# Input projection by block products: the forget gate's place among the token sums, a later split of a11 − a21, and the pace of the attention steps

## The chip, the cores and the metric

The kernel runs on one core of a Trainium2 chip. The metric is the device time of one execution in microseconds (us), less is better; a kernel's time is the median over several runs. The engines are PE (TensorE, matrix products), DVE (VectorE), ACT (ScalarE), POOL (GpSimd) and SP (SyncE, which issues most transfers).

## What is computed

One decoder block over 512 tokens of width 2048, in float32. A gated linear attention (four heads) and a differential softmax attention (four heads) share one input projection; their concatenated results go through one output projection, and a gated MLP with a short convolution follows.

```python
proj = h @ w_in                                  # 512 x 2048 by 2048 x 6160
gq, gk, gv, gg, ga, dq, dk, dv = ...             # columns of proj
log_a = jax.nn.log_sigmoid(ga @ w_alpha_up + b_alpha) / GLA_TAU
o_a = gla_chunked(gq, gk, gv, log_a)             # 4 heads, chunks of 64 tokens
o_a = rmsnorm(o_a, gla_norm) * silu(gg)
o_b = diff_attention(dq, dk, dv, lam)            # 4 heads, query blocks of 128, causal
o_b = rmsnorm(o_b, diff_norm) * (1.0 - lambda_init)
m = concatenate([o_a, o_b]) @ w_o
x = x + rmsnorm(m, attn_post_norm)
x = x + rmsnorm(conv_ffn(rmsnorm(x, ffn_pre_norm)), ffn_post_norm)
```

## The kernel before

**Products.** Every float32 operand is held as two parts, a rounded high part and the rest. ACT copies to the high part and DVE subtracts to get the low part; a product is three matmuls (high by high, low by high, high by low). The normed tokens lie as `ah` and `al` for the whole phase. Weights come as granules of 128 x 1024 numbers (`raw`, 512 KB): `granule` copies one on ACT (L137) and subtracts it on DVE (L138) into one of the slots of `ring`, and PE then runs the granule's matmuls. `split` (L150 on ACT, L151 on DVE) does the same for tokens.

**Block products.** The first columns of the input projection (gv's first half, gq's and gk's first halves) are plain products (L173 to L175 for the last of them). The other columns go through ten units of 512 columns (`InUnit`). A unit views tokens and weights as 2 x 2 blocks and takes seven block products, in the order x0, z0, y0, z1, x1, y1, y2 (y2 after the next unit's x0), where four products use sums of token blocks and sums of weight blocks. A segment has two granules of 24 matmuls each of 256 columns (L695 to L697 or L699 to L701). The weight blocks `b22` of y0 and z1 are fetched into "rm" buffers by SP (L48), and L720 adds them on DVE to the blocks that z0 used.

**Token sums.** `in_sums` makes, for each of two halves of the tokens' blocks, q = s5 (used in z0), then s2 (y0) and s3 (z1) from it in place, and r = a11 − a21 (L416 to L418). These run on 128 x 1024 tiles on DVE. r's split (to `sums["s7"]`, for y1) overwrites the rows of `ah` and `al` that hold a21, so it must come behind all uses of a21. q, r, and `b22` are all "rm" tiles, of which there are two.

**Forget gate.** `forget_gate` loads 16 columns of weights (`gar`), splits them into `gas`, multiplies (L439, L440: 32 matmuls), copies to `gaT`, multiplies by the second weight (L448), and computes the log of the sigmoid for four heads: Abs (L452), Exp (L457) and Ln (L459) on ACT, minimum (L453) and subtraction (L462) and a running sum (L463, a scan) on DVE; the sums go to DRAM (`bcd`). Its four `za` tiles are 128 x 512, in the "qk" pool with four buffers.

**Fillers.** The attention work is written as generators in the list `fill`: `in_sums`, `forget_gate`, then `gla_head` (14 steps each) and `diff_head` (8 steps each: a load, then a pipeline of `probs`, `turn`, `values` and `store` over four query blocks). `step()` is called after each granule; it adds `pace[0]` to a counter and runs one step of the first generator for every whole number. `drain()` runs all that is left. In `gla_head` the matmuls L510 and L502 are the scores (L502 is called the level products below) and DVE's L489 to L495 make their operands. In `diff_head` L589 makes scores on PE, L605 ends the softmax on DVE, L612 transposes it, L614 copies it on ACT, L620 multiplies by the values, L623 and L626 norm the result, L632 transposes it and L634 copies it (`dst`).

**What sets the order.** Each engine runs its instructions in a fixed order. In this phase a scheduler sets it when the kernel is built: it takes the instructions in the order written, with a simulated time line, and may move an instruction ahead of one that waits. PE's queue is in order, so an attention product whose operand is late stops the granules behind it. Behind the last unit the output projection follows (L191 to L193), which begins with the slots of the differential heads (`place_diff`, split by L150 and L151) and takes the gate's slots (`turn_gate`, transposes L781) last.

Of the kernel before, what the change touches and what calls it, by code (L numbers as in the profile page):

```python
# [9 lines left out]
F32 = mybir.dt.float32  # L10
F32R = mybir.dt.float32r
U8 = mybir.dt.uint8
AF = mybir.ActivationFunctionType
# [4 lines left out]
P = 128  # L18
D = 2048
S = 512  # L20
# [15 lines left out]
def hybrid_layer(ctx: ExitStack, tc: tile.TileContext, x, attn_pre_norm, w_in, w_alpha_up, b_alpha,  # L36
# [10 lines left out]
    def dma(o, i):  # L47
        return nc.sync.dma_start(out=o, in_=i)  # L48
# [3 lines left out]
    act = nc.scalar.activation  # L52
# [20 lines left out]
    ah = const.tile([P, NT, KT, P], F32R, name="ah")  # L73
    al = const.tile([P, NT, KT, P], F32R, name="al")
    wpool = ctx.enter_context(tc.tile_pool(name="w", bufs=3))

    def bank(pool=None):
        return (pool or psa).tile([P, 512], F32, name="bank", tag="bank")

    fill = []  # L80
    pace = [0.0, 0.0]
# [67 lines left out]
    def split(hi, lo, src):  # L149
        act(hi, src, AF.Copy)  # L150
        tt(lo, src, hi.bitcast(F32), ALU.subtract)  # L151
# [44 lines left out]
    def proj_n(w3, col, emit, order=tuple(range(KT)), first=0, banks=None):  # L196
        if banks is None:
            banks = [bank(psm) for _ in range(NT)]
        for g in range(first, KT // 2):
            w = granule(w3[:, order[2 * g]:order[2 * g] + 2, col:col + 512], 2)  # L200
            for t in range(NT):
                mm_n(banks, t, g, w)
                if g == KT // 2 - 1:
                    emit(t, banks[t])
            step()
# [99 lines left out]
    HK = KT // 2  # L305
# [21 lines left out]
    def wide(name):  # L327
        return mx.tile([P, GR], F32, name=name, tag="rm", bufs=2)

    def block_tile(name):  # L330
        return mx.tile([P, 512], F32, name=name, tag="ub", bufs=5)

    def qk_tile(name):
        return mx.tile([P, S], F32, name=name, tag="qk", bufs=4)

    def tmp(name):
        return mx.tile([P, S], F32, name=name, tag="tmp", bufs=4)

    def quarter(name):
        return mx.tile([P, 256], F32, name=name, tag="w1", bufs=3)  # L340
# [6 lines left out]
    for li, hs in enumerate(LEVELS):  # L347
        nb = 64 // hs
        m = quarter("m")[:, :64]
# [38 lines left out]

    s7raw = []

    def in_sums():
        for i in range(2):
            def blk(r, c):
                return [v[:, 2 * r + i, HK * c:HK * (c + 1), :].bitcast(F32) for v in (ah, al)]

            a11, a12, a21, a22 = blk(0, 0), blk(0, 1), blk(1, 0), blk(1, 1)

            def flat(name):
                return wide(name).rearrange("p (k c) -> p k c", c=P)

            q = flat("q")
            tt(q, a21[0], a22[0], ALU.subtract)
            tt(q, q, a21[1], ALU.add)
            tt(q, q, a22[1], ALU.subtract)
            split(sums["s5"][0][:, i], sums["s5"][1][:, i], q)
            yield
            tt(q, q, a11[0], ALU.subtract)
            tt(q, q, a11[1], ALU.subtract)
            split(sums["s2"][0][:, i], sums["s2"][1][:, i], q)
            yield  # L410
            tt(q, q, a12[0], ALU.add)
            tt(q, q, a12[1], ALU.add)
            split(sums["s3"][0][:, i], sums["s3"][1][:, i], q)
            yield
            r = flat("r")
            tt(r, a11[0], a21[0], ALU.subtract)  # L416
            tt(r, r, a11[1], ALU.add)
            tt(r, r, a21[1], ALU.subtract)  # L418
            s7raw.append(r)
            yield  # L420

    def forget_gate():
        gar = quarter("gar").rearrange("p (k r) -> p k r", r=RANK)
        dma(gar, w_in3[:, :, C_GA:C_GA + RANK])
        gas = mx.tile([P, KT, 80], F32R, name="gas", tag="v", bufs=1)
        nc.gpsimd.memset(gas.bitcast(F32), 0.0)
        split(gas[:, :, 0:RANK], gas[:, :, 64:64 + RANK], gar)
        wup = block_tile("wup")[:80, :]
        nc.gpsimd.memset(wup, 0.0)
        dma(wup[0:RANK, :], w_alpha_up[0])  # L430
        dma(wup[64:64 + RANK, :], w_alpha_up[0])
        keep = block_tile("keep")
        nc.gpsimd.memset(keep, 1.0)
        nc.gpsimd.memset(keep.rearrange("p (c x) -> p c x", c=4)[:, :, 0:1], 0.0)
        yield
        gab = bank()
        gav = gab[:80, :].rearrange("p (t c) -> p t c", c=P)
        for k in range(KT):
            mm(gav, gas[:, k, :], ah[:, :, k, :], start=k == 0, stop=False)  # L439
            mm(gav, gas[:, k, :], al[:, :, k, :], start=False, stop=k == KT - 1)  # L440
        gaT = block_tile("gaT")[:80, :]
        nc.vector.tensor_copy(gaT, gab[:80, :])
        yield

        za, bt = [], []
        for h in range(GH):
            zb = bank()
            mm(zb, wup[:, h * P:(h + 1) * P], gaT, start=True, stop=True)  # L448
            bcol = cols[:, h:h + 1]
            za.append(qk_tile("za"))  # L450
            bt.append(tmp("bt"))
            act(za[h], zb, AF.Abs, bias=bcol)  # L452
            ts(bt[h], zb, bcol, 0.0, ALU.add, ALU.min)  # L453
            if h % 2:
                yield
        for m in za:
            act(m, m, AF.Exp, scale=-1.0)  # L457
        for m in za:
            act(m, m, AF.Ln, bias=1.0)  # L459
        yield  # L460
        for h, m in enumerate(za):
            tt(m, bt[h], m, ALU.subtract)  # L462
            nc.vector.tensor_tensor_scan(bt[h], keep, m, 0.0, ALU.mult, ALU.add)  # L463
            dma(bcd[h], bt[h])
            if h % 2:
                yield
# [282 lines left out]
    def rows_unit(col, dst):  # L749
        def done(j, i, u):  # L750
            dma(dst[:, 2 * i:2 * i + 2, 256 * j:256 * (j + 1)], two(u))

        return InUnit(False, (col, col + 256), done)

    def pair_unit(c0, c1, d0, d1):
        def done(j, i, u):
            dma((d0, d1)[j][:, :, 256 * i:256 * (i + 1)], two(u))

        return InUnit(True, (c0, c1), done)
# [46 lines left out]
    def plain_out(d):  # L806
        def emit(n, b):
            u = block_tile("qk0")
            act(u, b, AF.Copy)
            dma(d[0][:, n, :], u)  # L810
        return emit

    units = [rows_unit(C_GV + 512, gvd[1]), pair_unit(C_GQ + 256, C_GK + 256, gqd[1], gkd[1])]
# [5 lines left out]
            units.append(pair_unit(C_DQ + 256 * h, C_DK + 256 * h, dqd[h], dkd[h]))  # L819
    units += [gate_unit(0), gate_unit(1)]  # L820

    fill.extend((in_sums(), forget_gate()))
    pace[0] = 1.35
    proj_n(w_in3, C_GV, gv_out, first=4, banks=banks)
    proj_t(w_in3, C_GQ, plain_out(gqd))
    banks = [bank(psm) for _ in range(2)]
# [6 lines left out]
        step()  # L833
    for n in range(2):
        plain_out(gkd)(n, banks[n])
    for i, r in enumerate(s7raw):
        split(sums["s7"][0][:, i], sums["s7"][1][:, i], r)
    fill.extend((gla_head(0), gla_head(1)))
    pace[:] = 0.62, 0.0
    units[0].z0()  # L840
    for i, u in enumerate(units):
        u.y0()
        u.z1()
# [23 lines left out]
    m = [wp.tile([P, D], F32, name=f"m{t}") for t in range(NT)]  # L867
# [722 lines left out]
```

## Time and profile before

| | us |
|---|---|
| runs | 2126.39, 2127.74, 2123.69 (median 2126.39) |
| profiled execution, its own time | 2123.57 |
| its span | 2121.9 |
| PE busy in the span | 2071.5 |
| DVE busy | 1539.2 |
| ACT busy | 988.8 |
| POOL busy | 287.8 |

The mean granted PE clock of the profiled execution is 0.994. Rows of a timeline give start, duration, engine, line, operation and tiles; a bracket at the end tells how long the engine was idle before the row and who ended that wait. Rows of the windows view give a stretch, its length, the busy time (and count) of PE, PE's weight loads, DVE, ACT and POOL, then PE's granted clock, the share of the DMA engines and GB/s. PE's matmuls overlap in the pipeline, so durations are longer than the distance between starts, which is what PE takes for one.

### The profile page before, as it was taken

How to read it: one execution, taken by the hardware profiler on the slowest of the kernel's cores; microseconds unless marked ns; L12 is line 12 of the kernel's file. 1: busy time of each engine (PE TensorE's matmuls, PEld its weight loads, DVE VectorE, ACT ScalarE, POOL GpSimd, SP SyncE). 2: the span in 40 equal slices, each digit the busy share in tenths (PEclk: the TensorE clock that was granted, in tenths of full speed). 3: DMA queues.
4: the chain of work that ended last, by engine and by line, in shares of the span. 5: the costliest groups of instructions: out<-in, count | busy, mean ns of one | idle time of the engine just before them, and what ended most of it. 6: DMA issues, size and time to landing. Idle time of an engine off the chain costs nothing.

```text
span 2121.9 us, 35562 instructions
## 1 busy us (share of the span) xinstructions
PE 2071.5 (98%) x14449; PEld 1907.2 (90%) x14449; DVE 1539.2 (73%) x1844; ACT 988.8 (47%) x1274; POOL 287.8 (14%) x306
## 2 busy tenths in 40 slices
PE   7999999999989999999999999999999999999998
PEld 6789999999967889899999999999999878787886
DVE  5867676666754246787786787878777778888887
ACT  4364444455653234344554544454444554444433
POOL 0212122222200000011111111111110110110100
PEclk9999999999999999999999999999999999999999
DMA  5567877898755345356757667577676876676653
GB/s 208 132 166 180 191 180 181 178 197 198 177 161 185 102 145 171 122 126 158 176 135 191 152 152 189 137 169 179 145 168 176 222 223 175 182 188 165 171 164 142
DMA packets 280697, 358.61 MB, mean 169 GB/s; under 512 B 14592, under 2 KB 221876, under 8 KB 278612
## 3 DMA queue, kind: packets, MB, share of 16 engines
q1 hardware_dynamic: 195732, 261.95, 36.6%
q0 software_dynamic: 84800, 94.38, 29.4%
q8 instruction: 113, 1.85, 0.4%
q14 instruction: 52, 0.43, 0.1%
HBM read 311.72 MB, written 44.56 MB: 168 GB/s over the span
## 4 chain that ended last, share of the span: by engine, by line
issue 54%; PE 34%; POOL 4%; DVE 3%; ACT 2%; DMA 2%; POOLq 0%; SPq 0%; DVEq 0%; ACTq 0%
PE bank L695 3%; PE bank L697 3%; PE bank L696 3%; PE bank L192 3%; PE bank L191 3%; PE bank L193 3%; PE bank L699 3%; PE bank L701 3%; PE bank L700 3%; POOL rt L1118 2%; POOL raw L1118 2%; PE bank L502 1%; DVE ring L138 1%; PE bank L589 1%; PE bank L175 1%
## 5 line engine op out<-in xcount | busy, mean ns | idle before, releaser
L137 ACT ACTIVATE ring<-raw 128x1024 fp32r<-128x1024 f32 x325 | 343.7, 1060 | 538.8 <-PE bank L1171 116.1
L138 DVE TENSOR_TENSOR ring<-raw,ring 128x1024 fp32r<-128x1024 f32 x325 | 395.6, 1221 | 230.9 <-ACT ring L137 230.7
L1172 PE MATMUL bank<-ah,ring 128*128 128x256 f32 x1280 | 353.5, 276 | 0.7 <-DVE ring L138 0.7
L1170 PE MATMUL bank<-ah,ring 128*128 128x256 f32 x1280 | 353.3, 276 | 0.0
L1171 PE MATMUL bank<-al,ring 128*128 128x256 f32 x1280 | 353.3, 276 | 0.0
L137 ACT ACTIVATE ring<-rt 128x1024 fp32r<-128x1024 f32 x221 | 233.0, 1059 | 226.8 <-PE bank L1171 143.8
L138 DVE TENSOR_TENSOR ring<-rt,ring 128x1024 fp32r<-128x1024 f32 x221 | 268.8, 1220 | 90.2 <-ACT ring L137 90.0
L1172 PEld LDWEIGHTS bank<-ah,ring 128*128 128x128 f32 x1280 | 240.2, 188 | 0.9 <-DVE ring L138 0.9
L1170 PEld LDWEIGHTS bank<-ah,ring 128*128 128x128 f32 x1280 | 240.2, 188 | 0.1
L1171 PEld LDWEIGHTS bank<-al,ring 128*128 128x128 f32 x1280 | 240.2, 188 | 0.1
L1273 PE MATMUL bank<-ring,ah 128*128 128x512 f32 x424 | 166.6, 393 | 4.3 <-DVE ring L138 4.2
L1274 PE MATMUL bank<-ring,al 128*128 128x512 f32 x424 | 165.2, 390 | 0.0
L1272 PE MATMUL bank<-ring,ah 128*128 128x512 f32 x424 | 159.0, 392 | 2.0 <-ACT ring L137 1.2
L191 PE MATMUL bank<-ring,ah 128*128 128x512 f32 x280 | 110.1, 399 | 4.0 <-ACT ah L150 3.9
L192 PE MATMUL bank<-ring,ah 128*128 128x512 f32 x280 | 110.5, 396 | 0.4 <-DVE ring L138 0.4
L193 PE MATMUL bank<-ring,al 128*128 128x512 f32 x280 | 108.1, 394 | 0.0
L1118 POOL DMA_DIRECT2D raw<-in_w_ffn_in_dram x40 | 51.0, 1278 | 405.4 <-DVE ring L138 402.5
L1273 PEld LDWEIGHTS bank<-ring,ah 128*128 128x128 f32 x424 | 79.6, 188 | 25.5 <-DVE ring L138 9.4
L1272 PEld LDWEIGHTS bank<-ring,ah 128*128 128x128 f32 x424 | 79.3, 188 | 21.6 <-ACT ring L137 4.9
L1118 POOL DMA_DIRECT2D rt<-in_w_ffn_in_dram x40 | 50.9, 1274 | 320.1 <-DVE ring L138 258.4
L1274 PEld LDWEIGHTS bank<-ring,al 128*128 128x128 f32 x424 | 79.6, 188 | 16.3
L695 PE MATMUL bank<-ah,ring 128*128 128x256 f32 x320 | 91.4, 285 | 0.0
(348 smaller groups left out, 5680.7 us busy)
## 6 DMA issues: line engine op xcount, KB each, us to landing
raw<-in_w_ffn_in_dram SPq DMA_DIRECT2D x96, 512.0 KB, 5.4
raw<-in_w_in_dram SPq DMA_DIRECT2D x56, 512.0 KB, 5.8
raw<-in_w_ffn_out_dram SPq DMA_DIRECT2D x48, 512.0 KB, 5.9
raw<-in_w_in_dram POOLq DMA_DIRECT2D x40, 512.0 KB, 6.7
rt<-in_w_ffn_in_dram SPq DMA_DIRECT2D x40, 512.0 KB, 6.1
rt<-in_w_ffn_in_dram POOLq DMA_DIRECT2D x40, 512.0 KB, 6.1
raw<-in_w_ffn_in_dram POOLq DMA_DIRECT2D x40, 512.0 KB, 7.7
raw<-in_w_o_dram SPq DMA_DIRECT2D x32, 512.0 KB, 4.0
```

The source lines that it names most:

```text
L137: act(hi, raw, AF.Copy)
L138: tt(lo, raw, hi.bitcast(F32), ALU.subtract)
L191: mm(banks[t], ah[:, t, s, :], w[0][:, k, :], start=st, stop=False)
L192: mm(banks[t], ah[:, t, s, :], w[1][:, k, :], start=False, stop=False)
L193: mm(banks[t], al[:, t, s, :], w[0][:, k, :], start=False, stop=sp)
L1118: nc.gpsimd.dma_start(out=raws[g].rearrange("p (a b) -> p a b", a=self.a), in_=self.block(0, j, g), accum_op=ALU.add)
L1170: mm(o, wh, sh[:, :, kk, :], start=start and kk == 0 and n == 0, stop=False, **NOW)
L1171: mm(o, wh, sl[:, :, kk, :], start=False, stop=False, **NOW)
L1172: mm(o, wl, sh[:, :, kk, :], start=False, stop=kk == HK - 1, **NOW)
L1272: mm(b[j], sh[:, o:o + P], w[0][:, q, :], start=start and st == 0, stop=False, **NOW)
L1273: mm(b[j], sh[:, o:o + P], w[1][:, q, :], start=False, stop=False, **NOW)
L1274: mm(b[j], sl[:, o:o + P], w[0][:, q, :], start=False, stop=st == 3, **NOW)
```

## The change

`in_sums` is cut in two: `first_sums` makes s5 and s2, `last_sums` makes s3 and r. `forget_gate` stands first in `fill`, ahead of both. Its four `za` tiles become halves of two 128 x 1024 tiles from the "rm" pool, so that Exp and Ln run as two instructions each. The pace of the first phase goes from 1.35 to 1.6, that of the attention steps from 0.62 to 0.75. The split of r moves from ahead of the first unit's z0 to behind it. Lines from `forget_gate`'s logs on stand 7 further down in the changed kernel (L720 becomes L727, L589 becomes L596, and so on).

```diff
--- before.py
+++ after.py
@@ -388,16 +388,18 @@
 
     s7raw = []
 
-    def in_sums():
+    def flat(name):
+        return wide(name).rearrange("p (k c) -> p k c", c=P)
+
+    def in_blocks(i):
+        return [[v[:, 2 * r + i, HK * c:HK * (c + 1), :].bitcast(F32) for v in (ah, al)]
+                for r in range(2) for c in range(2)]
+
+    s3raw = []
+
+    def first_sums():
         for i in range(2):
-            def blk(r, c):
-                return [v[:, 2 * r + i, HK * c:HK * (c + 1), :].bitcast(F32) for v in (ah, al)]
-
-            a11, a12, a21, a22 = blk(0, 0), blk(0, 1), blk(1, 0), blk(1, 1)
-
-            def flat(name):
-                return wide(name).rearrange("p (k c) -> p k c", c=P)
-
+            a11, a12, a21, a22 = in_blocks(i)
             q = flat("q")
             tt(q, a21[0], a22[0], ALU.subtract)
             tt(q, q, a21[1], ALU.add)
@@ -407,7 +409,12 @@
             tt(q, q, a11[0], ALU.subtract)
             tt(q, q, a11[1], ALU.subtract)
             split(sums["s2"][0][:, i], sums["s2"][1][:, i], q)
+            s3raw.append(q)
             yield
+
+    def last_sums():
+        for i, q in enumerate(s3raw):
+            a11, a12, a21, a22 = in_blocks(i)
             tt(q, q, a12[0], ALU.add)
             tt(q, q, a12[1], ALU.add)
             split(sums["s3"][0][:, i], sums["s3"][1][:, i], q)
@@ -442,21 +449,21 @@
         nc.vector.tensor_copy(gaT, gab[:80, :])
         yield
 
-        za, bt = [], []
+        zs = [wide("za") for _ in range(2)]
+        za, bt = [z[:, h * S:(h + 1) * S] for z in zs for h in range(2)], []
         for h in range(GH):
             zb = bank()
             mm(zb, wup[:, h * P:(h + 1) * P], gaT, start=True, stop=True)
             bcol = cols[:, h:h + 1]
-            za.append(qk_tile("za"))
             bt.append(tmp("bt"))
             act(za[h], zb, AF.Abs, bias=bcol)
             ts(bt[h], zb, bcol, 0.0, ALU.add, ALU.min)
             if h % 2:
                 yield
-        for m in za:
-            act(m, m, AF.Exp, scale=-1.0)
-        for m in za:
-            act(m, m, AF.Ln, bias=1.0)
+        for z in zs:
+            act(z, z, AF.Exp, scale=-1.0)
+        for z in zs:
+            act(z, z, AF.Ln, bias=1.0)
         yield
         for h, m in enumerate(za):
             tt(m, bt[h], m, ALU.subtract)
@@ -819,8 +826,8 @@
             units.append(pair_unit(C_DQ + 256 * h, C_DK + 256 * h, dqd[h], dkd[h]))
     units += [gate_unit(0), gate_unit(1)]
 
-    fill.extend((in_sums(), forget_gate()))
-    pace[0] = 1.35
+    fill.extend((forget_gate(), first_sums(), last_sums()))
+    pace[0] = 1.6
     proj_n(w_in3, C_GV, gv_out, first=4, banks=banks)
     proj_t(w_in3, C_GQ, plain_out(gqd))
     banks = [bank(psm) for _ in range(2)]
@@ -833,11 +840,11 @@
         step()
     for n in range(2):
         plain_out(gkd)(n, banks[n])
+    fill.extend((gla_head(0), gla_head(1)))
+    pace[:] = 0.75, 0.0
+    units[0].z0()
     for i, r in enumerate(s7raw):
         split(sums["s7"][0][:, i], sums["s7"][1][:, i], r)
-    fill.extend((gla_head(0), gla_head(1)))
-    pace[:] = 0.62, 0.0
-    units[0].z0()
     for i, u in enumerate(units):
         u.y0()
         u.z1()
```

The first place is DVE at the forget gate's logs and the token sums. Before, all sums are made by here, the gate's logs (L453, L462, L463) end, and r's splits (`al<-r`) and the sum with `b22` (L720) follow:

```order
L453 TENSOR_SCALAR bt<-bank,cols 128x512
L463 SCALAR_TENSOR_TENSOR bt<-keep,za 128x512
L453 TENSOR_SCALAR bt<-bank,cols 128x512
L462 TENSOR_TENSOR za<-bt,za 128x512
L463 SCALAR_TENSOR_TENSOR bt<-keep,za 128x512
L462 TENSOR_TENSOR za<-bt,za 128x512 x2
L463 SCALAR_TENSOR_TENSOR bt<-keep,za 128x512 x2
L138 TENSOR_TENSOR ring<-raw,ring 128x1024
L151 TENSOR_TENSOR al<-r,ah 128x1024 x2
L138 TENSOR_TENSOR ring<-raw,ring 128x1024 x2
L720 TENSOR_TENSOR raw<-raw,b_1120 128x1024
```

After, on the same engine, the gate's rows (L449 to L470) stand ahead of and between the first rows of the token sums (L404 to L406, the tile q):

```order
L449 COPY gaT<-bank 80x512
L460 TENSOR_SCALAR bt<-bank,cols 128x512 x4
L469 TENSOR_TENSOR za<-bt,za 128x512 x2
L470 SCALAR_TENSOR_TENSOR bt<-keep,za 128x512 x2
L138 TENSOR_TENSOR ring<-raw,ring 128x1024
L404 TENSOR_TENSOR q<-ah 128x1024
L469 TENSOR_TENSOR za<-bt,za 128x512 x2
L405 TENSOR_TENSOR q<-q,al 128x1024
L138 TENSOR_TENSOR ring<-raw,ring 128x1024
L470 SCALAR_TENSOR_TENSOR bt<-keep,za 128x512 x2
L406 TENSOR_TENSOR q<-q,al 128x1024
L404 TENSOR_TENSOR q<-ah 128x1024
```

The gate's subtractions and scans moved from behind the last r to the start of the token sums. Further on, after the changed kernel's first split of r, DVE has the last row of the second r (L425), the first head's operands (`d`, `qe`), the first use of `b22` (L727, and L138 on `b_1114`) and the second r's split (L151):

```order
L425 TENSOR_TENSOR r<-r,al 128x1024
L500 TENSOR_TENSOR qe<-d,gq 128x256
L502 TENSOR_TENSOR d<-d,gk 128x4x64
L727 TENSOR_TENSOR raw<-raw,b_1114 128x1024
L518 TENSOR_TENSOR sc<-bank,ident 128x512
L500 TENSOR_TENSOR qe<-d,gq 128x256
L502 TENSOR_TENSOR d<-d,gk 128x8x32
L138 TENSOR_TENSOR ring<-b_1114,ring 128x1024
L500 TENSOR_TENSOR qe<-d,gq 128x256
L502 TENSOR_TENSOR d<-d,gk 128x16x16
L502 TENSOR_TENSOR d<-d,gk 128x32x8
L151 TENSOR_TENSOR al<-r,ah 128x1024
```

Before, both splits stood directly behind one ring subtraction and ahead of both sums with `b22`; now the second one stands behind the first sum with `b22`.

The second place is PE at the end of the input projection. Before, the last differential head's rows (`s`, `dk`, `dvt`, `on`) up to the output projection (L191):

```order
L612 MATMUL bank<-ident,s 128x128
L589 MATMUL bank<-dk,dq 128x256 x2
L620 MATMUL bank<-dvt,aT 128x256
L612 MATMUL bank<-ident,s 128x128 x2
L589 MATMUL bank<-dk,dq 128x384 x2
L632 MATMUL bank<-ident,on 128x128 x2
L620 MATMUL bank<-dvt,aT 128x256 x2
L612 MATMUL bank<-ident,s 128x128 x3
L589 MATMUL bank<-dk,dq 128x512 x2
L632 MATMUL bank<-ident,on 128x128 x2
L620 MATMUL bank<-dvt,aT 128x256 x3
L191 MATMUL bank<-ring,ah 128x512
```

After, at the last differential head's last query block, ahead of the segment y1 of the last unit (L706 to L708):

```order
L708 MATMUL bank<-ring,ah 128x256
L619 MATMUL bank<-ident,s 128x128 x4
L639 MATMUL bank<-ident,on 128x128 x2
L627 MATMUL bank<-dvt,aT 128x256 x4
L639 MATMUL bank<-ident,on 128x128 x2
L706 MATMUL bank<-ring,ah 128x256
L707 MATMUL bank<-ring,al 128x256
L708 MATMUL bank<-ring,ah 128x256
```

The rows of three query blocks of that head, which stood without a granule between them, now stand at earlier places among the units' granules, and four transposes, four value products and two stores' transposes remain in one piece.

## The prediction

> **What bounds the kernel now.** I read the page first: PE (TensorE matmuls) is busy for 98% of the span, so an edit is worth only what it does to the few stretches in which PE idles or runs at a lower clock. Those I looked for in the windows view, which gives the busy time of each engine per stretch, with PE's granted clock in the third column from the right. The stages around the change read:
>
> ```profile
> 100.00:120.00 20.00, 18.14 (x96) 14.45 (x94) 13.29 (x15) 16.27 (x20) 1.29 (x1) 0.99 0.40 96
> 120.00:140.00 20.00, 17.94 (x91) 15.03 (x90) 13.57 (x16) 9.73 (x13) 1.27 (x1) 0.84 0.57 185
> 140.00:580.00 440.00, 440.00 (x3648) 432.73 (x3646) 305.40 (x485) 219.85 (x346) 101.88 (x111) 1.00 0.85 187
> ...
> 600.00:620.00 20.00, 11.14 (x31) 6.43 (x30) 11.88 (x36) 9.34 (x27) 1.48 (x4) 0.78 0.24 72
> 620.00:640.00 20.00, 19.63 (x88) 16.09 (x87) 9.22 (x19) 10.95 (x21) 0.74 (x2) 0.97 0.48 151
> 640.00:660.00 20.00, 16.07 (x79) 13.00 (x78) 9.66 (x14) 7.37 (x14) 1.60 (x2) 0.91 0.45 139
> ```
>
> Stretch minus busy time times clock is what a stage loses. At the front that is 20 − 18.14 × 0.99 = 2.0 and 20 − 17.94 × 0.84 = 4.9, so 7 us. At the tail of the input projections it is 20 − 11.14 × 0.78 = 11.3, 20 − 19.63 × 0.97 = 1.0 and 20 − 16.07 × 0.91 = 5.4, so 17.7 us. The 440 us between lose nothing, with DVE (VectorE) busy for 69% of them. So about 25 us are to be had here, and nothing else of the span is touched by the diff.
>
> **Front: why PE waits.** PE's timeline at 117 us:
>
> ```profile
> 117.31 0.28 PE L701 MATMUL bank<-ring,ah 128*128 128x256 f32 x1
> 119.45 0.74 PE L173 MATMUL bank<-ah,ring 128*128 128x512 f32 x1 [1.86 <-ACT ring L137]
> 119.99 0.63 PE L174 MATMUL bank<-al,ring 128*128 128x512 f32 x1
> 122.67 0.80 PE L175 MATMUL bank<-ah,ring 128*128 128x512 f32 x1 [2.06 <-DVE ring L138]
> 123.27 0.63 PE L173 MATMUL bank<-ah,ring 128*128 128x512 f32 x1
> 123.69 0.63 PE L174 MATMUL bank<-al,ring 128*128 128x512 f32 x1
> ```
>
> It waits twice for the two halves of one weight granule (ring), 3.9 us in all, and the matmuls behind the waits start 0.42 us apart. ACT (ScalarE) and DVE, which make those halves, stand in the forget gate's logs:
>
> ```profile
> 106.55 1.28 ACT L459 ACT_TABLE_LOAD   x1
> ...
> 116.00 1.28 ACT L459 ACT_TABLE_LOAD   x1
> 117.30 1.15 ACT L459 ACTIVATE za<-za 128x512 f32<-128x512 f32 x2
> 118.35 1.04 ACT L137 ACTIVATE ring<-raw 128x1024 fp32r<-128x1024 f32 x1
> ```
>
> ```profile
> 117.96 1.29 DVE L462 TENSOR_TENSOR za<-bt,za 128x512 f32<-128x512 f32 x2 [1.93 <-ACT za L459]
> 119.17 2.33 DVE L463 TENSOR_TENSOR_SCAN bt<-keep,za 128x512 f32<-128x512 f32 x2
> 121.42 1.20 DVE L138 TENSOR_TENSOR ring<-raw,ring 128x1024 fp32r<-128x1024 f32 x1
> ...
> 128.92 1.23 DVE L720 TENSOR_TENSOR raw<-raw,b 128x1024 f32<-128x1024 f32 x1 [1.76 <-DMA b<-in_w_in_dram]
> ```
>
> From 106.55 to 118.35 ACT alternates between Exp (L457) and Ln (L459) and loads a table five times (the first and the last load are shown). DVE's last two scans then stand ahead of the ring subtraction that PE needs.
>
> The Trainium skill says ("ScalarE: Activation LUTs", Table sets) that one set holds both exp and ln, by which there would be one load and little for the change to save here. The trace speaks against that for this kernel: a 1.28 us load stands at each change of function. The same page (What ACT_TABLE_LOAD costs) puts 1.38 us of drain on top of each load; here the Ln at 117.30 starts 0.02 us after its load's end, so I count the load alone.
>
> **Front: what the change does.** The forget gate goes ahead of the sums, and its logs into two wide tiles: two Exp, then two Ln. It can start once its weights (gar) are there.
>
> ```profile
> 62.83 1.57 SPq L102 DMA_DIRECT2D raw<-in_w_in_dram  x2
> ```
>
> ```profile
> 70.93 0.38 SPq L48 DMA_DIRECT2D gar<-in_w_in_dram  x1
> ```
>
> ```profile
> b<-in_w_in_dram SPq DMA_DIRECT2D x2, 512.0 KB, 5.2
> ```
>
> ```profile
> gar<-in_w_in_dram SPq DMA_DIRECT2D x1, 128.0 KB, 4.9
> ```
>
> The two answers on transfers give 5.2 us from the issue to the landing of a b22 block and 4.9 for gar. By the order gar now stands behind the first weight load of the pair at 62.83, so it is sent at about 63, lands at 68 and is split at 68.5. PE takes 32 gate products, 18 others and four more (an estimate of 0.21 us each, half of the 0.42 above, 11.3 us, and 1 us from the last product to ACT), so the first za is written at about 81. Two wide Exp and Ln at the 1.04 us of L137 (same tile size), two table loads, and half of the subtractions and scans bring DVE to 91 or 92. All of this lies beside PE's work, and the wait at 117 goes: +7 us.
>
> What takes its place starts with a pool. The wide za tiles take the two buffers of the "rm" pool, which the sums' q, then r, then unit 0's two b22 weight blocks also use. So no sum can start before the scans, r (a11 − a21) comes behind the sums, and the b22 loads behind r's splits, which also stand behind z0 now. DVE has 36 rows in one unbroken run there, 33 of them wide. Their price is in DVE's timeline:
>
> ```profile
> 81.58 1.23 DVE L403 TENSOR_TENSOR q<-q,al 128x1024 f32<-128x1024 f32 x1
> 82.72 1.22 DVE L138 TENSOR_TENSOR ring<-raw,ring 128x1024 fp32r<-128x1024 f32 x1
> ```
>
> The two start 1.14 us apart and last 1.22 to 1.23. At 1.14 to 1.22 us each the wide ones take 38 to 40 us, the narrow subtractions and scans 4 more. So the first r split ends at 134 to 136, b22's first block lands 5.2 us later at 139.5 to 141.5, and DVE needs four more operations (the sum with b22 of L720, three short ones, then the ring subtraction, 4 us) before the product can go on: 143.5 to 145.5. PE, meanwhile:
>
> ```profile
> 140.62 0.28 PE L699 MATMUL bank<-ring,in_s2h 128*128 128x256 f32 x1
> ...
> 153.72 0.28 PE L699 MATMUL bank<-ring,ah 128*128 128x256 f32 x1
> ...
> 156.55 1.00 PE L502 MATMUL bank<-qe,d 128*128 128x64 f32 x8
> ```
>
> Before, z0 ends at 140.62 and z1 at 153.72, with one group of level products (L502) among them. After, PE is 7 us earlier at z0's end (133.7). It has only the head's first products to do there (1.2 us) and then waits some 9 us for b22. Then come two half segments (2.8 us each), and the second b22 block, which is sent after the second r split (2.4 us behind the first block's subtraction), lands 5.2 us later and needs 3.5 us more: 154.5 to 157. With two more half segments and the level products between, z1 ends at 161 to 164, plus 1 to 2 us of half clock behind the waits. Six more of the 1.00 us level groups are done by then than before, so the fair mark of before is 153.72 + 6 = 159.7. Net of the 7 us gained, the front **loses 4 us**. The bounds: PE may find the second block landed already and DVE ahead (a gain of 7, the old wait gone and nothing new), or the chain may stretch (a loss of 16, third rival).
>
> **Middle.** Pace 0.62 to 0.75 puts 21% more attention steps beside each granule. DVE's 69% holds 55% of weight splitting, so attention grows from 14% to 17%: 72%. No row of before shows a wait in 440 us, so the cover holds on average; where an attention product stands in PE's queue ahead of its operand it costs the wait. I take 1 us, between 0 and 5. That the steps themselves cost PE more is excluded: they are the same steps.
>
> **Tail: what the change does.** Before, 7 of the last differential head's 8 steps are left when the generators are drained, and PE runs them with nothing between:
>
> ```profile
> 599.57 0.61 PE L589 MATMUL bank<-dk,dq 128*128 128x128 f32 x4
> 604.41 0.47 PE L612 MATMUL bank<-ident,s 128*128 128x128 f32 x1 [4.23 <-DVE s L605]
> ```
>
> ```profile
> 655.87 0.80 PE L191 MATMUL bank<-ring,ah 128*128 128x512 f32 x1 [3.52 <-ACT ah L150]
> ```
>
> Each of three blocks waits on PE for its softmax on ACT and DVE (the 4.23 us is the first), and the head's late result is what the output projection waits for at 655.87. With the denser pace, the order has products between all blocks but the last. There four transposes, four value products and the two stores' transposes stand in a row ahead of y1, which needs ACT's copy of an earlier result, queued behind the store's copy. Its links are priced by
>
> ```profile
> 614.76 0.38 ACT L623 ACTIVATE jk<-bank 128x256 f32<-128x256 f32 x1
> ```
>
> ```profile
> 616.43 0.48 DVE L626 SCALAR_TENSOR_TENSOR on<-bank,rs,dnb 128x256 f32<-128x256 f32 x1
> ```
>
> From the square's start to the normed block's end is 2.15 us. Around it stand transposes (0.6), ACT's copy of them (0.75), value products (2.2), the stores' transposes and copy (0.9) and the late copy with its latency (1): 7.6 us, of which PE works 3.2. With 1.7 us of half clock behind it 6 us stay lost, and 0.5 us of small waits. The tail **gains 17.7 − 6.5 = 11 us**, between 6 (two such chains) and 15 (ACT's copy comes early).
>
> The Trainium skill ("TensorE: Matmul & The Clock Gate", Part 1) has the clock halve only after an idle window of about 3.4 us. The rows at 119.45 show matmuls 0.42 us apart after 1.86 us of idle time, so I charge half clock behind the shorter waits too; by the rule the second wait for b22, if it is under 3.4 us, would halve nothing and the front would lose 1 us less.
>
> **Sum.** 11 − 4 − 1 = 6 us faster: the profiled execution's 2123.6 becomes 2117.6. The profiled execution lay 2.8 us under the median of the runs (2126.4), so I predict a median of **2120**.
>
> **Rivals.**
> - *The front's wait goes and nothing takes its place.* The order lets PE keep the 7 us, if the sums are done 8 us sooner than I count. For it: DVE idles before the scans. Against it: the pool, which forbids the sums that time. With the tail's 11 to 15 and the middle's 1 it is a gain of 13 to 19: 2107 to 2113. Chance 0.15.
> - *The gains cancel.* The tail's own chain stays longer (6 us gained) and the front loses 4 to 6: a change of 0 to 4 us, some runs slower, 2122 to 2131. Chance 0.20.
> - *Slower: unit 0 waits longer on the "rm" chain than the tail gives.* DVE at 1.26 us instead of 1.17 (3 us over 33), two landings 2.5 us longer beside the other loads (5), half clock over 44 matmuls (0.1 each, 4) on top of 4 make a loss of 16 at the front; less a tail of 10, and 1 for the middle, it is 7 slower: 2133, or 2131 to 2136. It decides from the point where the front loses more than the 10 us that the tail gives, that is when b22's second block lands after about 158. Chance 0.20.
> - *The change doesn't do what it says:* by the order it does, on each engine; no chance given.
>
> **How the numbers follow.** My own case (0.45) spans 2114 to 2125. A measurement of this kernel can tell about 0.2%, 4.3 us, from no change: below 2122.1 counts as faster, above 2130.6 as slower. Faster: 0.36 of my case and 0.15 of the first rival, 0.51. Same: 0.09 and 0.13 of the second, 0.22. Slower: 0.07 and 0.20, 0.27. The range from 2109 to 2135 leaves out the best of the first rival and the worst of the third; my case alone would have 2114 to 2125.
>
> **What would show it.** Right: no wait of PE's at 117 us, ACT's log block about 80 to 90 us with two table loads, the first sum on DVE only behind the scans at 91, a wait of PE's for b22 from about 135, of 6 us or more; 140 to 580 with PE still busy throughout; not three waits for L605 in the last head, but one of about 4 us ahead of y1 there, and none of 3.5 us in the output projection. Wrong: sums that start before the scans, b22 landed before z0's end, or waits in the middle of more than 5 us together.

## The result, and the profile after

The changed kernel takes 2127.7 us (median of 12 runs, 2123.89 to 2130.86) against 2125.89 us (12 runs) before: a ratio of 1.0007, 95% interval 0.9995 to 1.0018. That is no change within what a measurement of this kernel can tell. The profiled executions are 2123.57 us before and 2125.11 us after. The forecast was 2120 us, 0.3% faster, with a range that holds the result; the time is that of the second rival, the gains that cancel.

The windows view of the changed kernel, with the columns as before (stretch, its length, busy PE, PE loads, DVE, ACT, POOL, then PE's clock):

```profile
100.00:120.00 20.00, 20.00 (x113) 17.50 (x112) 20.00 (x19) 10.97 (x13) 2.74 (x2) 1.00 0.68 154
120.00:140.00 20.00, 15.96 (x99) 14.37 (x97) 20.00 (x26) 9.73 (x15) 0.00 (x0) 0.92 0.35 106
140.00:160.00 20.00, 19.25 (x137) 18.77 (x137) 18.24 (x34) 9.19 (x12) 5.05 (x4) 0.82 0.71 136
...
580.00:600.00 20.00, 14.92 (x84) 13.24 (x83) 10.16 (x22) 8.73 (x17) 2.60 (x3) 0.83 0.67 154
600.00:620.00 20.00, 9.59 (x67) 8.15 (x65) 11.53 (x18) 12.51 (x23) 2.06 (x4) 0.95 0.48 136
620.00:640.00 20.00, 18.66 (x130) 17.87 (x131) 15.88 (x22) 12.25 (x19) 0.00 (x0) 0.88 0.76 250
640.00:660.00 20.00, 20.00 (x96) 16.67 (x95) 6.96 (x9) 4.76 (x6) 0.00 (x0) 1.00 0.70 257
```

With the same sum as in the prediction (stretch minus busy time times clock) the front, 100 to 160 us, loses 0 + 5.3 + 4.2 = 9.5 us, where it lost 7. The tail, 580 to 660 us, loses 7.6 + 10.9 + 3.6 + 0 = 22.1 us, where it lost 18.5 (17.7 from 600 us on). Between 160 and 580 us PE is busy throughout, as before.

At the front the wait at 117 us is gone and the forecast one has come, at 4.0 us where I had some 9. PE's timeline, with the start of the first head's products behind z0, the wait for b22's first block, and the first row behind z1:

```profile
133.75 1.05 PE L517 MATMUL bank<-gq,gk 128*128 128x128 f32 x8
138.84 0.58 PE L706 MATMUL bank<-ring,in_s3h 128*128 128x256 f32 x1 [4.04 <-ACT ring L137]
...
161.38 0.28 PE L706 MATMUL bank<-ring,ah 128*128 128x256 f32 x1
```

DVE's timeline there gives the first split of r, the use of b22's first block and of its second:

```profile
131.16 1.23 DVE L151 TENSOR_TENSOR al<-r,ah 128x1024 fp32r<-128x1024 f32 x1
...
137.93 1.22 DVE L727 TENSOR_TENSOR raw<-raw,b 128x1024 f32<-128x1024 f32 x1
...
149.37 1.23 DVE L727 TENSOR_TENSOR raw<-raw,b 128x1024 f32<-128x1024 f32 x1 [1.52 <-DMA b<-in_w_in_dram]
```

The tail has no gain. These are PE's waits between 580 and 660 us, after (first) and before:

```profile
PE bank L706 <- ACT ring L137: 5.1, 2, 3.4
PE bank L706 <- ACT u L731: 4.2, 1, 4.2
PE bank L639 <- DVE on L633: 3.8, 1, 3.8
PE bank L708 <- DVE ring L138: 2.8, 2, 1.7
PE bank L627 <- ACT aT L621: 0.9, 1, 0.9
```

```profile
PE bank L612 <- DVE s L605: 9.6, 4, 4.2
PE bank L191 <- ACT ah L150: 3.9, 2, 3.5
PE bank L192 <- DVE ring L138: 0.4, 1, 0.4
```

The columns are the total, the number of waits and the longest. The softmax waits of the last head and the output projection's wait are gone, as forecast (13.9 us of waits), and 16.8 us of other waits stand in their place: for weight granules, for the copy of a unit's block (u) and for the head's normed block (on).

The first granule wait (3.36 us, up to 586.24) is ACT's queue: ACT is busy without a break from 581.63, with the head's exponentials and the gate's sigmoid behind a table load, and only then copies the granule:

```profile
582.96 1.28 ACT L774 ACT_TABLE_LOAD   x1
...
585.14 1.04 ACT L137 ACTIVATE ring<-raw 128x1024 fp32r<-128x1024 f32 x1
```

ACT's timeline at the last wait, that for u:

```profile
610.85 1.28 ACT L774 ACT_TABLE_LOAD   x1
612.14 0.63 ACT L774 ACTIVATE sg<-p 128x512 f32<-128x512 f32 x1
...
617.18 0.38 ACT L641 ACTIVATE dst<-bank 128x256 f32<-128x256 f32 x1 [2.15 <-PE bank L639]
620.69 0.60 ACT L731 ACTIVATE u<-bank 128x512 f32<-128x512 f32 x1 [3.13 <-DMA ogd<-p]
```

The copy of the unit's block, on which y1 waits, doesn't wait for ACT's queue alone, as I had priced it. It needs one of the five result buffers ("ub"), and that is still being read by a store of the gate's result (ogd), which SP sent at 614.87 and which takes 5.8 us:

```profile
614.87 0.42 SPq L48 DMA_DIRECT2D ogd<-p  x1
```

```profile
ogd<-p SPq DMA_DIRECT2D x1, 256.0 KB, 5.8
```

### The profile page after: what moved, and what is told of

It reads as the page before. It is cut to its first block, busy times and chain, and to the rows that moved or that the text cites. A ratio compares the mean times of both kernels' runs of the same rounds, so it can differ in the third digit from the quotient of the medians.

```text
span 2123.4 us, 35558 instructions
## 1 busy us (share of the span) xinstructions
PE 2070.1 (97%) x14449; PEld 1911.3 (90%) x14449; DVE 1537.4 (72%) x1844; ACT 980.9 (46%) x1264; POOL 281.0 (13%) x306
## 4 chain that ended last, share of the span: by engine, by line
PE 52%; issue 36%; DVE 6%; POOL 3%; DMA 2%; ACT 1%; POOLq 0%; SPq 0%; DVEq 0%; ACTq 0%
PE bank L1178 5%; PE bank L1179 5%; PE bank L1177 5%; PE bank L191 3%; PE bank L192 3%; PE bank L193 3%; PE bank L702 3%; PE bank L704 3%; PE bank L703 3%; PE bank L708 3%; PE bank L706 3%; PE bank L707 3%; DVE ring L138 1%; POOL rt L1125 1%; PE bank L175 1%
## 5 line engine op out<-in xcount | busy, mean ns | idle before, releaser
L138 DVE TENSOR_TENSOR ring<-raw,ring 128x1024 fp32r<-128x1024 f32 x325 | 395.9, 1221 | 242.8 <-ACT ring L137 237.7
L1179 PE MATMUL bank<-ah,ring 128*128 128x256 f32 x1280 | 353.4, 276 | 0.1
L1177 PE MATMUL bank<-ah,ring 128*128 128x256 f32 x1280 | 353.3, 276 | 0.0
L138 DVE TENSOR_TENSOR ring<-rt,ring 128x1024 fp32r<-128x1024 f32 x221 | 269.0, 1221 | 91.9 <-ACT ring L137 91.7
L191 PE MATMUL bank<-ring,ah 128*128 128x512 f32 x280 | 109.0, 396 | 0.0
L706 PE MATMUL bank<-ring,ah 128*128 128x256 f32 x320 | 92.8, 290 | 9.4 <-ACT ring L137 5.1
L708 PE MATMUL bank<-ring,ah 128*128 128x256 f32 x320 | 93.0, 291 | 2.8 <-DVE ring L138 2.8
```

Source lines behind the costliest of these rows:

```text
L138: tt(lo, raw, hi.bitcast(F32), ALU.subtract)
L191: mm(banks[t], ah[:, t, s, :], w[0][:, k, :], start=st, stop=False)
L708: mm(o, sh[:, n, kk, :], wl[:, k, :], start=False, stop=sp_, **NOW)
L1177: mm(o, wh, sh[:, :, kk, :], start=start and kk == 0 and n == 0, stop=False, **NOW)
L1179: mm(o, wl, sh[:, :, kk, :], start=False, stop=kk == HK - 1, **NOW)
```

## The experiments

Theory A is that the front loses a little (the shared "rm" buffers) and the tail gains nothing, because at pace 0.75 its work meets ACT's queue, which also holds the gate units' sigmoids and copies. Theory B is that the tail gained what I forecast and the front lost it. Each kernel was timed in five rounds beside the kernel before.

**1. The pace alone.**

```diff
 # the kernel before
-    pace[:] = 0.62, 0.0
+    pace[:] = 0.75, 0.0
```

> The kernel before with the pace of the attention steps at 0.75 and nothing else changed. Theory A (the tail did not gain: with 0.75 the last differential head still ends inside the last unit, where each of its steps waits for an ACT queue that also holds the gate's sigmoids and copies): the tail loses about 22 us as in the changed kernel, the front 7 as before, so 2126 + 4 = 2130 us, with PE waits for ACT and DVE from 580 us on. Theory B (the tail gained the 11 us forecast, and the front lost them): 2115 us, with about 6.5 us lost in the tail.

Measured: a ratio of 1.0028 (1.0015 to 1.0041), 6 us slower. The windows of its tail:

```profile
580.00:600.00 20.00, 14.91 (x85) 13.21 (x85) 8.38 (x20) 9.63 (x18) 1.63 (x3) 0.83 0.62 144
600.00:620.00 20.00, 9.49 (x61) 7.89 (x60) 13.55 (x20) 11.84 (x23) 2.06 (x4) 0.83 0.53 154
620.00:640.00 20.00, 13.94 (x85) 13.12 (x84) 11.73 (x17) 7.76 (x13) 0.00 (x0) 0.76 0.70 214
```

They lose 7.6 + 12.1 + 9.4 = 29 us. Theory B falls: the pace of 0.75 by itself makes the tail worse. It does so by more than in the changed kernel (22 us), for which I have only the later waits of its output projection (for a granule, 2.8 us, and for the gate's blocks, 3.2 us) and no cause.

**2. The front alone.**

```diff
 # the changed kernel
-    pace[:] = 0.75, 0.0
+    pace[:] = 0.62, 0.0
```

> The changed kernel with the pace of the attention steps back at 0.62: gate first, wide logs, split sums, later split of a11 - a21. Theory A: the front costs 2 to 3 us net (9.5 us lost against 7, from the windows) and the tail is as before, so 2128 us. Theory B: the front costs some 12 us, 2138 us.

Measured: 1.0012 (0.9998 to 1.0026), 2.5 us, as theory A has it, though the interval includes no change. Its front loses 9.1 us and its tail 18 us, the tail of before.

**3. The wide log tiles out of the shared buffers.**

```diff
 # the changed kernel; s3's tiles are allocated in last_sums under the same tag
-        zs = [wide("za") for _ in range(2)]
+        room = sp.tile([P, 2 * GR], F32, name="za", tag="s3h")
+        zs = [room[:, GR * i:GR * (i + 1)] for i in range(2)]
```

> The changed kernel with the two wide log tiles in the place that the sum s3 takes later, not in the buffers that the sums' q, r and the b22 loads share; all else as changed, pace 0.75. If those shared buffers make the wait at 134 us, the sums run before the logs on DVE, the b22 blocks land before z0 ends, PE has no wait of over 1 us between 100 and 160 us, and the time falls by about 9 us from the changed kernel's: 2119 us. If DVE's amount of work makes that wait, wherever the tiles are, it stays at 4 us or more and the time is 2127 us.

Measured: 1.0045 (1.0032 to 1.0058), 9.6 us slower than before where I had expected 7 us faster. The wait for b22 is gone: no wait of PE's is left between 100 and 160 us. PE is late in this run (z0 ends at 144.2 us), which would hide a part of such a wait; but SP sends the b22 blocks at 125.42, where the changed kernel sends them from 132.42 on, and in experiment 8, where z0 ends at 138.0, the wait is gone as well. So the shared buffers made it. But two new ones stand earlier:

```profile
72.18 0.23 PE L381 MATMUL bank<-ident,ba 4*128 4x4 f32 x1 [4.51 <-issue]
76.58 0.71 PE L447 MATMUL bank<-ah,gas 128*80 128x512 f32 x1 [3.59 <-DVE gas L151]
```

```profile
72.44 0.37 SPq L48 DMA_DIRECT2D gar<-in_w_in_dram  x1
```

The first stands ahead of the transposes of small rows; the view names no releaser, but one of those rows (ba) was sent at 68.98, behind three weight loads, where it left at 61.94 in the changed kernel. The second is for the gate's weights, which leave at 72.44, behind the same loads (62.38 in the changed kernel). With half clock behind them the two waits cost 11 us between 60 and 80 us. The tail, at 29 us, is that of the first run. In the changed kernel, where the sums could not run yet, the gate's weights came in time; that the early sums alone put the weight loads ahead of them is argued from these rows, not tested.

**4. A pace of 0.85**, on the changed kernel and on the kernel before.

```diff
-    pace[:] = 0.75, 0.0     # 0.62 in the kernel before
+    pace[:] = 0.85, 0.0
```

> The changed kernel with the pace at 0.85 in place of 0.75. By the order the last head's blocks then all have products between them, and only its last store stands alone. If the last head's place makes the tail's loss, that falls from 22 us to about 8 and the time to 2114 us, with the middle still without a wait. If denser attention costs elsewhere (DVE at 75% between 140 and 580 us), waits of 5 us or more show there and the time is 2125 us or over.

> The kernel before with the pace of the attention steps at 0.85 and nothing else changed. If the whole gain of 0.85 comes from the tail and the changed front is worth nothing or costs a little (9.5 us lost against 7), this is as fast as 0.85 with the changed front or 2 us faster: a ratio to before of 0.996 to 0.997, 2120 us. If the gain needed the changed front, the ratio is 0.999 or more.

Measured: 0.9972 (0.9962 to 0.9983) with the changed front and 0.9970 (0.9958 to 0.9981) with the front of before. The tail's windows of the former:

```profile
580.00:600.00 20.00, 17.64 (x129) 16.87 (x128) 12.62 (x21) 14.54 (x22) 6.05 (x6) 0.91 0.77 157
600.00:620.00 20.00, 16.81 (x114) 16.14 (x113) 13.38 (x19) 10.54 (x18) 1.16 (x2) 0.84 1.01 274
620.00:640.00 20.00, 20.00 (x135) 18.35 (x134) 13.75 (x18) 9.97 (x16) 0.00 (x0) 0.99 0.63 195
```

They lose 3.9 + 5.9 + 0.2 = 10 us, and those of the other kernel 10.2. So 0.85 brings in the tail most of what I forecast of 0.75, at a cost of 2.4 us of waits in the middle (for the heads' loads), and the changed front adds nothing. The time falls by 6 us, half of the 12 that I had expected.

**5. Six result buffers**, with a control.

```diff
 # the changed kernel, pace 0.75; the control leaves the first pair of lines out
-        return mx.tile([P, 512], F32, name=name, tag="ub", bufs=5)
+        return mx.tile([P, 512], F32, name=name, tag="ub", bufs=6)
-        return mx.tile([P, 256], F32, name=name, tag="w1", bufs=3)
+        return mx.tile([P, 256], F32, name=name, tag="w1", bufs=2)
-        return mx.tile([P, GDV], F32, name=name, tag="jk", bufs=3)
+        return mx.tile([P, GDV], F32, name=name, tag="jk", bufs=2)
```

> The changed kernel (pace 0.75) with six buffers in place of five for the units' results (ub), and two in place of three for the attention's row tiles and quarter tiles, which pay for the room. If the tail loses its time because the copy of a unit's block waits for a buffer that a gate store still reads, the copies wait for no store, PE's waits for u and for on at 611 to 621 us go, and the tail loses some 12 us less: 2116 us. If the last head's late place alone makes it, the tail still loses about 20 us and the time is 2127 us; a loss of over 3 us in the middle would come from the two smaller pools.

> The control of the run with six result buffers: the changed kernel with two row and two quarter tiles in place of three each, and still five result buffers. If the sixth result buffer made that run's gain, this one is as slow as the changed kernel or slower: the tail loses 20 us or more, 2127 us or over, a ratio to before of 1.000 or more. If the smaller pools or the order that they bring made it, the ratio is 0.996 to 0.998.

Measured: 0.9964 (0.9952 to 0.9977) with six buffers, and 1.0031 (1.0020 to 1.0042) for the control. The tail's windows with six:

```profile
580.00:600.00 20.00, 20.00 (x146) 18.21 (x146) 13.52 (x25) 11.01 (x20) 3.91 (x4) 1.00 0.89 204
600.00:620.00 20.00, 17.05 (x120) 16.05 (x119) 14.40 (x23) 14.97 (x25) 2.17 (x4) 0.91 0.49 152
620.00:640.00 20.00, 18.16 (x98) 15.13 (x97) 14.19 (x21) 11.08 (x19) 0.24 (x1) 1.00 0.76 245
```

They lose 0 + 4.5 + 1.8 = 6.3 us, near the 6.5 that I had forecast for the tail of 0.75, but not through the chain that I had priced: PE's waits are 2.6 us for the last softmax and 1.8 us for a stored block of the gate. ACT's wait for a store there falls to 1.0 us:

```profile
ACT u L731 <- DMA ogd<-u: 1.0, 1, 1.0
```

In the control it is longer than in the changed kernel:

```profile
ACT u L731 <- DMA ogd<-p: 5.7, 1, 5.7
ACT aT L621 <- PE bank L619: 5.4, 2, 4.5
```

The control's tail loses 22.3 us, as much as the changed kernel's. So the gain needs the sixth buffer. The smaller pools cost something at the front: between 60 and 160 us the control loses 12.6 us and the run with six buffers 11.0, against 9.5, and PE waits 2.8 and 2.5 us there for the gate's weights, which leave at 65.4 and 65.6.

The buffer also changed the order that the scheduler made: with five it drew 24 matmuls of a later segment ahead of z1 and left the last block's rows bare; with six z1 stands whole and the last block's rows have products between them. Most of the gain came with the order. The store alone holds ACT's copy for 3.1 us; in the control it holds it for 5.7, and yet PE waits no longer for that copy than in the changed kernel (4.0 us, against 4.2). The waits for granules (7.9 us) and for the normed block (3.8 us) are for no store, and with six buffers they are gone too. A result buffer may still be the reason for the order: the copy that z1 needs (L722) waits for a store with five and runs at 588.61, and with six it runs at 578.16. That the scheduler drew the other segment forward for this was not tested.

**6. No sigmoid in the gate.**

```diff
 # the changed kernel
-            act(sg, u, AF.Sigmoid)
+            act(sg, u, AF.Copy)
```

> The changed kernel with the gate's sigmoid replaced by a copy (so the result leaves out the gate's sigmoid); the order on PE is the same, but ACT has no table loads between the gate's and the last head's functions. If those loads (1.28 us each, three or more of them between 580 and 625 us) make the tail's waits, the tail loses 4 to 5 us less: 2123 us. If buffers make them, it changes by 1 us or less.

Measured: 0.9993 (0.9980 to 1.0006), 3 us under the changed kernel with overlapping intervals; its tail loses 17.1 us, 5 less. The wait for the block's copy stays (4.0 us). So ACT's table loads seem to be a part of the tail's loss, 5 us by the windows, and not the larger one.

**7. Six buffers on the kernel before.** The edit is that of 5.

> The kernel before (pace 0.62) with the six result buffers and the two smaller pools. At 0.62 the last head still has seven steps left when the generators are drained, so a buffer can't help: the tail loses 18 us and the ratio is 0.998 to 1.002. If a free buffer is what the tail wants at any pace, the tail loses 8 us or less and the ratio is 0.995.

Measured: 0.9999 (0.9986 to 1.0012). Its tail loses 20.9 us and still waits for the last head's softmax, so at this pace the sixth buffer brings nothing:

```profile
PE bank L612 <- DVE s L605: 10.4, 4, 4.1
PE bank L191 <- ACT ah L150: 5.3, 2, 3.9
```

**8. The gate between the sums.**

```diff
 # with the log tiles as in 3, at pace 0.85
-    fill.extend((forget_gate(), first_sums(), last_sums()))
+    fill.extend((first_sums(), forget_gate(), last_sums()))
```

> Pace 0.85, the wide log tiles in the place of s3, and the fillers in the order first sums (s5, s2), forget gate, last sums. Its gate products stand on PE behind those of the kernel with the tiles apart and ahead of those before. If the front's loss is made only by PE's two waits (for the gate's late weights when the gate stands first, for b22 when the tiles share buffers), no wait of over 1 us is left between 40 and 160 us, some 9 us less than with 0.85 and the changed front: a ratio to before of 0.993, 2113 us. If the front's loss only moves again, a wait of 4 us or more shows at another place there and the ratio is 0.997.

Measured: 0.9954 (0.9940 to 0.9968), with a front that loses 3.7 us (60 to 160 us). One wait of over 1 us is left between 100 and 160 us:

```profile
120.61 0.50 PE L175 MATMUL bank<-ah,ring 128*128 128x512 f32 x1 [1.76 <-DVE ring L138]
```

That is 4 us less than at 0.85 with the changed front (0.9972; the intervals overlap a little), where I had expected 9: I had put the whole of the front's loss down to the two waits, and its windows give 6 (9.6 to 3.7).

**9. Both ends together.** The front of 8 and the buffers of 5.

> Both mended ends together: the logs in the place of s3 between first and last sums (front 3.8 us lost in the windows), six result buffers at pace 0.75 (tail 6.3 us lost, middle none). Against the 25.5 us that the kernel before loses this leaves 10 us: 15 us faster, a ratio to before of 0.993, 2113 us. If the two gains share a cause they don't add up, and the ratio stays at 0.9955.

> The same at pace 0.85, where the last head stands earlier. The front loses 3.8 us, the tail about 6 if the buffer helps there too (10 if it does not, since at 0.85 the copies wait less for a buffer), the middle 2.5 for the heads' loads that come late: 12 to 16 us lost, 10 to 13 us faster than before, a ratio of 0.994 to 0.9955, so no better than 0.75 with the buffer.

Measured: 0.9930 (0.9917 to 0.9942) at 0.75, 2115.2 us against 2129.9 us beside it, and 0.9952 (0.9937 to 0.9968) at 0.85. The former is the fastest of all the kernels here, 15 us under the kernel before. Its tail loses 6.4 us:

```profile
580.00:600.00 20.00, 20.00 (x154) 18.74 (x153) 13.20 (x25) 12.05 (x20) 2.61 (x3) 1.00 0.78 183
600.00:620.00 20.00, 16.44 (x100) 15.34 (x100) 14.14 (x23) 14.14 (x26) 2.41 (x4) 0.83 0.59 183
620.00:640.00 20.00, 20.00 (x106) 16.68 (x105) 14.53 (x21) 11.22 (x19) 0.00 (x0) 1.00 0.69 228
```

Its front loses 7.7 us and not 3.7, through a wait that the front of 8 did not have, for the first head's operand:

```profile
PE bank L519 <- DMA gk<-gkd: 2.9, 1, 2.9
```

That the ratio is the 0.993 forecast is in part luck: its windows lose 14.1 us against 25.5, 11 us less, and the other 4 us of the 15 do not show in them. At 0.85 the sixth buffer brings nothing that the times show: 0.9952, against 0.9954 in experiment 8 without it.

## Why the prediction was right in its range and wrong in its likeliest case

- **Where PE loses.** Right. Every kernel that moved the time moved the windows at 60 to 160 or 580 to 660 us.
- **The front's old wait.** Right: the 7 us went, and z0 ends at 133.75 us against the 133.7 forecast.
- **The front's new wait.** Right in its mechanism, the "rm" chain (experiments 3 and 8 took the wait away), but less than half as long: PE waited 4.0 us, where I had some 9 and named 6 or more as the sign. I had b22's first block ready for DVE at 139.5 to 141.5 and it was used at 137.93, since r's first split ended at 132.4 and not at 134 to 136. And the first product behind the wait is not y0's, with four DVE operations ahead of it, but z1's (in_s3h at 138.84), which needs ACT's copy of the block first. z1 ends at 161.38, in the 161 to 164 forecast. The loss net of the old one is 2.5 us by the windows, where I had 4; experiment 2 gives the same, within an interval that includes no loss. ACT's logs took three table loads (84.36, 86.73 and 90.05) and not two, since the order has an Exp between the two Ln.
- **The middle.** Forecast 1 us, measured none at 0.75; at 0.85 it is 2.3 to 2.4. The working was wrong even so: DVE's ring splits (L138) are 161 us of the 440, 37% and not 55% (42% with the sums of b22), and DVE did not grow busier (289.25 us between 160 and 580 us before, 289.51 after), where I had it go from 69% to 72%.
- **The tail: the step that failed.** I had 17.7 − 6.5 = 11 us gained; it lost 3.6. "With the denser pace, the order has products between all blocks but the last" was true, and the old waits went. What failed is the sum of 6.5 us for what takes their place, and each of its terms measured more. The small waits, 0.5 us in the sum, are 7.9 us: ACT's copies of the granules stand in its queue behind the head's and the gate's work, and DVE's halves follow them. The idle time of the one chain, 7.6 − 3.2 = 4.4 us, is 8.9 us: 0.9 for the transposes' copy, 3.8 for the normed block and 4.2 for the late copy of the unit's block, which I had at 1 us "with its latency" and which ACT started 3.1 us late because no result buffer was free. The rest of the 22.1 us, 5.3 us, is half clock, where I had 1.7. The sum left out what else stands in ACT's queue and who holds the buffer that an instruction writes. One buffer more, with the order that it brings, leaves 6.3 us; how much each of the two is worth stays open.
- **The rivals.** The time is that of the second, with 0.20, and "the tail's own chain stays longer" is its mechanism. But its sum did not come: it had 6 us gained in the tail and 4 to 6 lost at the front, and the tail lost 3.6 and the front 2.5. That the two make a time within its 2122 to 2131 is luck. The slower rival named the front; by experiment 1 the slower outcome lay in the tail.
- **Not settled.** The windows add up to 6 us lost and the profiled time grew by 1.5. By its first product the MLP starts 3.6 us later (905.4 to 909.0) and its last product 1.3 us later (2067.5 to 2068.8), though its code is the same; which of its waits differ from run to run was not tried.

## What to carry to other kernels

When a filler's pace is raised, price the place where its last pieces land: there list for each instruction not only the operand that it reads but the buffer that it writes and the transfer that still reads it. A step of pace in the same direction can lose and then win (0.62, 0.75, 0.85 give 0, +6 and −6 us on the kernel before), so one value says little. And a change that moves work to the head of a queue is worth what its data's arrival allows: with the gate first, its weights left at 62.38 us in the changed kernel and PE did not wait for them, at 65.6 with the smaller pools and PE waited 2.5 us, at 72.44 in experiment 3 and PE waited 3.6 us.

## What the hardware showed that I had not expected

I charged half clock behind every wait of about 2 us. In the changed kernel PE waits 1.75 us at 604.89 and 1.12 us at 606.51, and the matmuls behind start 0.12 us apart, at full rate:

```profile
604.89 0.38 PE L706 MATMUL bank<-ring,ah 128*128 128x256 f32 x1 [1.75 <-ACT ring L137]
...
606.51 0.39 PE L708 MATMUL bank<-ring,ah 128*128 128x256 f32 x1 [1.12 <-DVE ring L138]
606.73 0.28 PE L706 MATMUL bank<-ring,ah 128*128 128x256 f32 x1
606.85 0.28 PE L707 MATMUL bank<-ring,al 128*128 128x256 f32 x1
```

After the waits of 3.36 and 1.72 us at 586 to 588 us they start 0.21 us apart, and after the two of 1.86 and 2.06 us in the kernel before also at half rate. In experiment 8 a single wait, the 1.76 us at 120.61, is followed by matmuls of 512 columns 0.42 us apart, again half rate:

```profile
121.44 0.63 PE L175 MATMUL bank<-ah,ring 128*128 128x512 f32 x1
121.86 0.63 PE L173 MATMUL bank<-ah,ring 128*128 128x512 f32 x1
```

So the length of a wait alone does not decide: 1.75 us left the full rate and 1.76 us did not. The rule of the Trainium skill ("TensorE: Matmul & The Clock Gate", Part 1), that the clock halves only after an idle window of about 3.4 us, agrees with the first pair, and with the second as far as 3.36 us is about that. The pair in the kernel before and the single wait of experiment 8 have no idle stretch near that length and went to half rate all the same. What decides is not shown here.
